# Column sums of squares in a hybrid encoder: fp32 products against split float32r ones

## The chip, the cores and the metric

The kernel runs on one core of a Trainium2 chip, all in float32 or float32r (fp32 data that TensorE multiplies in one pass, with fewer bits of mantissa). The metric is the time of one execution on the device in microseconds (us); for the kernel before it is the median of three runs, for the profiles a single execution.

## What is computed

An encoder trunk of two layers over 512 tokens of 1024 features. Cut to what matters:

```python
def rmsnorm(x, w):
    y = x * lax.rsqrt(jnp.mean(x * x, axis=-1, keepdims=True) + 1e-6)
    return y * w

for i in range(2):
    h = rmsnorm(x, norm_mix[i])
    x = x + (gla_mixer(h) if i == 0 else attn_mixer(h))
    x = x + conv_ffn(rmsnorm(x, norm_ffn[i]))

# inside attn_mixer: 8 query heads and 2 key heads of 128 features
q = apply_rope(rmsnorm(q, q_norm)); k = apply_rope(rmsnorm(k, k_norm))
```

So there are four norms over the 1024 features of a token (GLA's, the first feed-forward's, the attention's, the second feed-forward's), and norms over the 128 features of each query and key head. Each needs the sum of squares over features for every token. The output is x after both layers.

## The kernel before, in words

Activations lie with features on the 128 partitions and the 512 tokens along the free dimension: x is eight tiles of 128x512. Every weight product is made from a high and a low part: a value a is copied into float32r (hi, on ACT), the rest a - hi is written as float32r (lo, on DVE), and three one-pass products, hi by hi, hi by lo and lo by hi, take the place of an fp32 one (mm3, L555 to 559, and the loops at L610, L667, L735, L1155). The loops run over chunks of 128 input features (k or KC), output tiles, and, in most of the feed-forward, over the seven products of a Strassen scheme (L1155).

Four stages follow one another: gla, ffn(0), attention, ffn(1). What TensorE, ACT, DVE and GpSimd (POOL) do, and in which order, is written as one Python program; the framework underneath puts every instruction into its engine's queue when the kernel is built. It goes by the place in the program (earlier is more urgent) and by its own estimates of durations: an instruction is placed when its inputs are ready by the estimate and its engine is free, and another that is ready can be placed ahead of one that isn't. On the chip each queue then runs in the order so fixed. The kernel pushes the order where it matters with a table of actions by step (PLAN, tick), issue_after and high_priority. Tiles of one tag share a few buffers; the tag sq has three of 128x512, and a new tile waits until a buffer is free.

A norm (class Norm, L501 to 553) works in pieces. square (L529 to 536) squares a chunk of x on ACT (L531) and adds it on DVE (L535) into the tile ss, an sq buffer. tokens (L538 to 547) sums ss over the partitions: four blocks of 128 tokens are the stationary operand, one after the other, and a column of 1/1024 (ones, L476) is the moving one, so that 128 tokens' means come out as one column of PSUM (tile ms, L543). Then EPS is added on DVE (L487), the power -1/2 is taken on POOL (L491), and DVE copies it (rtok, L547). rows (L549 to 553) turns it into a tile R with one value for each token along the free dimension by four transposes (L498). In GLA tokens is the action T at step f3 and rows the action R at f6, while products for the first q and k tiles run.

In the attention (from L1441) the heads of q and k are made in pairs by roped (L1464 on): 8 + 8 steps of products into two PSUM tiles A and B, squares of both on ACT (L1470, L1471, tiles qa and qb in sq buffers), their sum on DVE (L1472), the rotation on DVE and POOL (L1480, L1499, L1500), and scale_tok (L1453 to 1462), which sums these squares (of both halves of a head's features) over the 64 partitions of each of the two heads: four blocks are stationary, and a two-column matrix bd with 1/128 in the upper half of one column and in the lower half of the other moves (tile hs, L1457). EPS is added on DVE (L1459) and POOL takes the root (L1461). The k pair runs first, then the norm's tokens, then the first q pair; the other three q pairs are spread over the steps of the attention's main loop, among scores (tile s), transposes of the probabilities (tile pt, L1623), products with v (po) and the output projection (op, L610). av (L584) are v's own products.

So the sums over partitions are made in 4 norms x 4 blocks and in 5 head pairs x 4 blocks, all with fp32 operands.

Of the kernel before, what the change touches and what calls it, by code (L numbers as in the profile page):

```python
# [8 lines left out]
F32 = mybir.dt.float32  # L9
F32R = mybir.dt.float32r  # L10
U8 = mybir.dt.uint8
AF = mybir.ActivationFunctionType
ALU = mybir.AluOpType

P = 128
S = 512
D = 1024
KC = D // P
NT = S // P
# [3 lines left out]
QH, HD = 8, 128  # L23
# [95 lines left out]
def hybrid_encoder_kernel(  # L119
# [23 lines left out]
    pe, act, dve, pool, sync = nc.tensor, nc.scalar, nc.vector, nc.gpsimd, nc.sync  # L143
    mm = pe.matmul

    cp = ctx.enter_context(tc.tile_pool(name="cp", bufs=1))
    sp = ctx.enter_context(tc.tile_pool(name="sp", bufs=1))
# [5 lines left out]
    def nm(s):  # L153
        uid[0] += 1
        return f"{s}{uid[0]}"
# [3 lines left out]
    def bank(tag, n):  # L159
        return pp.tile([P, S], F32, tag=tag, bufs=PS[tag], name=nm(n))  # L160
# [10 lines left out]
    def tiny(w, n, tag="tiny"):  # L171
        return sp.tile([P, 8], F32, tag=tag, bufs={"tiny": 36, "tiny2": 4}[tag], name=nm(n))[:, :w]
# [300 lines left out]
        mm(warm[:, :P], two[:, :P], two[:, P : 2 * P], start=i in (0, WARM - 8), stop=i in (WARM - 9, WARM - 1))  # L473
    halfneg = cp.tile([P, 8], F32, name="halfneg")
    dve.tensor_copy(halfneg, warm[:, :8])
    ones = cp.tile([P, 1], F32, name="ones")  # L476
    dve.memset(ones, 1.0 / D)
    bd = cp.tile([P, 2], F32, name="bd")
    dve.memset(bd, 0.0)
    dve.memset(bd[0:64, 0:1], 1.0 / HD)  # L480
    dve.memset(bd[64:128, 1:2], 1.0 / HD)

    def rsqrt_eps(src, w, n, scale=None, tag="tiny"):

        t = tiny(w, n, tag)
        if scale is None:
            dve.tensor_scalar(t, src, EPS, None, ALU.add)  # L487
        else:
            dve.tensor_scalar(t, src, scale, EPS, ALU.mult, ALU.add)
        r = tiny(w, n, tag)  # L490
        pool.tensor_tensor(r, t, halfneg[:, :w], ALU.pow)  # L491
        return r

    def bcast_rows(cols):

        ps = bank("po", "bc")
        for j in range(NT):
            pe.transpose(ps[:, j * P : (j + 1) * P], cols[j], ident)  # L498
        return ps

    class Norm:  # L501
# [36 lines left out]
        def tokens(self):  # L538

            assert self.done == KC  # L540
            ps = bank("po", "ms")
            for j in range(NT):
                mm(ps[:, j : j + 1], self.ss[:, j * P : (j + 1) * P], ones, start=True, stop=True)  # L543
            self.ms = ps[:, :NT]
            r = rsqrt_eps(self.ms, NT, "rtok")
            self.rtok = cp.tile([P, NT], F32, name=nm("rtok"))
            dve.tensor_copy(self.rtok, r)  # L547
# [92 lines left out]
    def gla(norm, nxt):  # L640
# [349 lines left out]
        def roots(h):  # L990

            oss = tiny(4, "oss")
            for s in range(NT):
                junk = tmp("sq", "junk", DV)
                act.activation(junk, O[h][:, s * DV : (s + 1) * DV], AF.Square, accum_out=oss[:, s : s + 1])
            ORS[h] = rsqrt_eps(oss, NT, "ors", 1.0 / DV)
# [444 lines left out]
    def attention(norm, nxt):  # L1441
# [11 lines left out]
        def scale_tok(sq, by, keep):  # L1453

            ps = bank("acc", "hs")
            for j in range(NT):
                mm(ps[:, 2 * j : 2 * j + 2], sq[:, j * P : (j + 1) * P], bd, start=True, stop=True)  # L1457
            t = tiny(8, "hs", "tiny2")
            dve.scalar_tensor_tensor(by_two(t), by_two(ps[:, :8]), by, by_block(eps[by]), ALU.mult, ALU.add)  # L1459
            o = cp.tile([P, 8], F32, name=nm(keep))  # L1460
            pool.tensor_tensor(o, t, halfneg, ALU.pow)  # L1461
            return o

        def roped(i, wcol, by, keep, tag="acc"):  # L1464
# [17 lines left out]
            turned(0)  # L1482
            yield
            sc = scale_tok(qa, by, keep)
            yield
            turned(1)
# [72 lines left out]
        ps = [bank("acc" if j < 2 else "pt", "av") for j in range(NT)]  # L1559
# [8 lines left out]
        for j in range(NT):  # L1568
            sl = slice(j * 256, (j + 1) * 256)
# [83 lines left out]
        for t in range(len(blocks) + LAG2):  # L1653
# [10 lines left out]
            if t >= LAG + 1 and (t - LAG) % 2 == 1 and t < len(blocks) + LAG:  # L1664
                h, j = blocks[t - LAG]
# [110 lines left out]
```

## Time and profile before

| what | value |
|---|---|
| median of 3 runs | 1073.53 us (1072.96 to 1073.98) |
| the profiled execution, its own time | 1074.18 us |
| its span, first to last instruction | 1072.5 us |
| granted TensorE clock | 1.00 |

The span lacks about 1.7 us of start and end that the time has. In the profile, PE is TensorE's matmuls, PEld its weight loads, DVE VectorE, ACT ScalarE, POOL GpSimd, SP the queue of SyncE; L543 is line 543 of the kernel. A row of the timeline has start and length in us, the engine, the line, the operation, output and inputs, shapes, and in brackets the idle time ahead of it and what ended that. A row with x8 stands for eight instructions in a run, from the first one's start to the last one's end. Ends of matmuls are modelled, and matmuls overlap: of two in a row, the distance of their starts is what counts. A row of waits has the total in us, how often, and the longest. Rows by tile have the shortest, the median and the longest duration in ns and the first and the last start in us.

### The profile page before, as it was taken

The numbers are of one execution on the slowest core, as the hardware profiler recorded it, in microseconds if no ns is written. First come the engines' busy times: TensorE is split into PE (matmuls) and PEld (weight loads), VectorE is DVE, ScalarE is ACT, GpSimd is POOL, SyncE is SP. The second block draws the span as 40 slices with busy tenths as digits, with TensorE's granted clock in tenths as the row PEclk, the third lists the DMA queues.
The fourth block names the chain that finished last, engine by engine and source line by source line (L and its number), as shares of the span: only waits on it lengthen the run. The fifth ranks groups of instructions, "written<-read, shape, count | busy, mean of one in ns | idle before, by whom it ended". The sixth has DMA issues, their size and how long they took to land.

```text
span 1072.5 us, 18688 instructions
## 1 busy us (share of the span) xinstructions
PE 1064.6 (99%) x7176; PEld 981.3 (91%) x7176; DVE 941.0 (88%) x1423; ACT 784.0 (73%) x1252; POOL 157.0 (15%) x169
## 2 busy tenths in 40 slices
PE   9999999999999999999999999999999999999998
PEld 8888988888999999999988888788899999999997
DVE  7998968878999999999985578787899999999996
ACT  8679665767886778776893677675888777876783
POOL 0212112021100110010015243001201021001000
PEclk9999999999999999999999999999999999999999
DMA  8744447666564874474768565486756487456562
GB/s 304 179 127 103 117 146 255 225 137 130 144 151 121 207 184 127 121 176 123 233 171 204 122 202 167 149 263 143 145 128 159 117 195 198 128 129 156 149 194 83
DMA packets 75323, 174.57 MB, mean 163 GB/s; under 512 B 6881, under 2 KB 7393, under 8 KB 75233
## 3 DMA queue, kind: packets, MB, share of 16 engines
q1 hardware_dynamic: 50624, 114.23, 31.8%
q0 software_dynamic: 19712, 50.60, 27.1%
q10 hardware_dynamic: 4896, 8.55, 2.2%
q8 instruction: 56, 0.92, 0.4%
q14 instruction: 35, 0.28, 0.1%
HBM read 124.85 MB, written 14.68 MB: 130 GB/s over the span
## 4 chain that ended last, share of the span: by engine, by line
PE 98%; ACT 1%; DVE 1%; DMA 0%; issue 0%; DVEq 0%; ACTq 0%
PE r L1155 53%; PE op L610 8%; PE vg L735 7%; PE up L558 3%; PE up L557 3%; PE up L559 3%; PE kq L667 2%; PE A L557 1%; PE A L559 1%; PE A L558 1%; PE B L557 1%; PE B L558 1%; PE B L559 1%; PE av L584 1%; PE pt L1623 1%; PE o L981 1%
## 5 line engine op out<-in xcount | busy, mean ns | idle before, releaser
L1155 PE MATMUL r<-xt,wh 128*128 128x256 f32 x1152 | 208.0, 282 | 0.0
L1155 PE MATMUL r<-gu,wh 128*128 128x256 f32 x1120 | 202.0, 283 | 0.0
L377 DVE TENSOR_TENSOR wl<-raw,wh 128x1024 fp32r<-128x1024 f32 x146 | 176.4, 1219 | 19.3 <-ACT wh L376 18.8
L1155 PEld LDWEIGHTS r<-xt,wh 128*128 128x128 f32 x1152 | 178.9, 190 | 0.2
L376 ACT ACTIVATE wh<-raw 128x1024 fp32r<-128x1024 f32 x146 | 151.1, 1051 | 33.6 <-PE vg L735 6.9
L1155 PEld LDWEIGHTS r<-gu,wh 128*128 128x128 f32 x1120 | 173.7, 191 | 1.1 <-ACT r L1224 0.3
L1155 PE MATMUL r<-xt,wl 128*128 128x256 f32 x576 | 162.8, 283 | 0.0
L1155 PE MATMUL r<-gu,wl 128*128 128x256 f32 x560 | 156.7, 283 | 0.0
L1155 PE MATMUL r<-nh,wh 128*128 128x256 f32 x432 | 122.5, 284 | 0.0
L1155 PE MATMUL r<-nh,wl 128*128 128x256 f32 x432 | 122.0, 283 | 0.0
L1155 PE MATMUL r<-nl,wh 128*128 128x256 f32 x432 | 121.7, 282 | 0.0
L1155 PEld LDWEIGHTS r<-xt,wl 128*128 128x128 f32 x576 | 109.7, 191 | 0.0
L1155 PEld LDWEIGHTS r<-gu,wl 128*128 128x128 f32 x560 | 106.3, 191 | 0.0
L1155 PEld LDWEIGHTS r<-nh,wh 128*128 128x128 f32 x432 | 82.1, 190 | 0.6
L1155 PEld LDWEIGHTS r<-nl,wh 128*128 128x128 f32 x432 | 82.1, 190 | 0.1
L1155 PEld LDWEIGHTS r<-nh,wl 128*128 128x128 f32 x432 | 82.1, 190 | 0.0
L376 ACT ACTIVATE wh<-sum 128x1024 fp32r<-128x1024 f32 x56 | 59.2, 1057 | 24.0 <-DVE sum L346 17.6
L610 PE MATMUL op<-oT,wh 128*128 128x512 f32 x256 | 72.6, 393 | 0.0
L377 DVE TENSOR_TENSOR wl<-sum,wh 128x1024 fp32r<-128x1024 f32 x56 | 68.3, 1219 | 3.8 <-ACT wh L376 3.8
L326 ACT ACTIVATE wh<-raw 128x1024 fp32r<-128x1024 f32 x46 | 48.3, 1051 | 18.0 <-PE A L558 6.7
L346 DVE TENSOR_TENSOR sum<-raw,raw 128x1024 f32<-128x1024 f32 x50 | 60.9, 1218 | 0.0
L610 PEld LDWEIGHTS op<-oT,wh 128*128 128x128 f32 x256 | 47.4, 188 | 9.7 <-ACT oT L1020 0.3
(304 smaller groups left out, 2579.3 us busy)
## 6 DMA issues: line engine op xcount, KB each, us to landing
raw<-in_w_up_dram SPq DMA_DIRECT2D x78, 512.0 KB, 5.2
raw<-in_w_down_dram SPq DMA_DIRECT2D x44, 512.0 KB, 4.1
wl<-raw POOLq DMA_DIRECT2D x20, 512.0 KB, 5.4
wl<-in_w_up_dram POOLq DMA_DIRECT2D x20, 512.0 KB, 6.6
ring<-p ACTq DMA_DIRECT2D x32, 256.0 KB, 2.4
xw<-in_xw_dram SPq DMA_DIRECT2D x8, 512.0 KB, 6.8
raw<-in_w_v_dram SPq DMA_DIRECT2D x8, 512.0 KB, 4.8
raw<-in_w_g_dram SPq DMA_DIRECT2D x8, 512.0 KB, 4.0
```

Of the source, the lines that this page charges most:

```text
L326: act.activation(hi, r, AF.Copy)
L346: dve.tensor_tensor(fold(e), t3[:, :S].rearrange("p (o n) -> p o n", o=1).to_broadcast([P, 2, S]), fold(tiles[0]), ALU.add)
L376: act.activation(hi[:, sl], a, AF.Copy)
L377: dve.tensor_tensor(lo[:, sl], a, hi[:, sl].bitcast(F32), ALU.subtract)
L557: mm(ps, wh, mh, start=start, stop=False, **kw)
L558: mm(ps, wh, ml, start=False, stop=False, **kw)
L559: return mm(ps, wl, mh, start=False, stop=stop, **kw)
L584: mm(ps[j][:, :width], hl[k][i == 2][:, j * P : (j + 1) * P], (wl if i == 1 else wh)[:, sl], start=k == 0 and i == 0, stop=k == KC - 1 and ...
L610: W.op = mm(pss[ng][n], wt[:, sl], mv, start=k == late[0][0] and i == 0, stop=k == late[-1][-1] and i == 2)
L667: mm(ps[t], (wl if i == 1 else wh)[:, kk * S + t * P : kk * S + (t + 1) * P], norm.hl[k][i == 2], start=k == 0 and i == 0, stop=k == KC - ...
L735: last = mm(ps[j], m[:, js], w[:, sl], start=i in (1, 7, 2) and p == 0 and a == 0, stop=i in (4, 2, 3) and p == 3 and a == 2, skip_group_c ...
L1155: mm(dst, w[:, sl], m, start=start and j == 0 and a == 0, stop=j == len(pairs) - 1 and a == 2, skip_group_check=True)
```

## The change

The columns ones and bd become parts of one float32r tile (a row of fp32 constants, bd0, is copied into it by one more operation on DVE; ones has two equal columns now). A new function column_sums splits a tile of sums of squares into high and low parts, in two sq buffers, and sums the two parts by two float32r products into the same two columns of PSUM, instead of one fp32 product. scale_tok uses it for all five head pairs; Norm.tokens uses it for the norms of even index, which are GLA's (0) and the attention's (2). The feed-forward norms (1 and 3) keep fp32 products. The means of a norm now lie in every second column of ms.

```diff
-    ones = cp.tile([P, 1], F32, name="ones")
-    dve.memset(ones, 1.0 / D)
-    bd = cp.tile([P, 2], F32, name="bd")
-    dve.memset(bd, 0.0)
-    dve.memset(bd[0:64, 0:1], 1.0 / HD)
-    dve.memset(bd[64:128, 1:2], 1.0 / HD)
+    bd0 = cp.tile([P, 4], F32, name="bd0")
+    dve.memset(bd0[:, 0:2], 1.0 / D)
+    dve.memset(bd0[:, 2:4], 0.0)
+    dve.memset(bd0[0:64, 2:3], 1.0 / HD)
+    dve.memset(bd0[64:128, 3:4], 1.0 / HD)
+    bd = cp.tile([P, 4], F32R, name="bd")
+    dve.tensor_copy(bd, bd0)
+    ones, bd = bd[:, 0:2], bd[:, 2:4]
...
+    def column_sums(ps, a, by):
+
+        hi, lo = (sp.tile([P, S], F32R, tag="sq", bufs=3, name=nm(n)) for n in ("sh", "sl"))
+        act.activation(hi, a, AF.Copy)
+        dve.tensor_tensor(lo, a, hi.bitcast(F32), ALU.subtract)
+        for j in range(NT):
+            for t in (hi, lo):
+                mm(ps[:, 2 * j : 2 * j + 2], t[:, j * P : (j + 1) * P], by, start=t is hi, stop=t is lo)
...
             ps = bank("po", "ms")
-            for j in range(NT):
-                mm(ps[:, j : j + 1], self.ss[:, j * P : (j + 1) * P], ones, start=True, stop=True)
-            self.ms = ps[:, :NT]
+            if self.idx % 2:
+                for j in range(NT):
+                    mm(ps[:, 2 * j : 2 * j + 1], self.ss[:, j * P : (j + 1) * P], bd0[:, 0:1], start=True, stop=True)
+            else:
+                column_sums(ps, self.ss, ones)
+            self.ms = ps[:, : 2 * NT : 2]
...
             ps = bank("acc", "hs")
-            for j in range(NT):
-                mm(ps[:, 2 * j : 2 * j + 2], sq[:, j * P : (j + 1) * P], bd, start=True, stop=True)
+            column_sums(ps, sq, bd)
```

## The prediction

> **What bounds the kernel now.** I read the page's busy times first, then its chain of waits, then the waits of TensorE, and then the stretches around the seven places that the change touches.
>
> ```profile
> PE 1064.6 (99%) x7176; PEld 981.3 (91%) x7176; DVE 941.0 (88%) x1423; ACT 784.0 (73%) x1252; POOL 157.0 (15%) x169
> PE 98%; ACT 1%; DVE 1%; DMA 0%; issue 0%; DVEq 0%; ACTq 0%
> ```
> ```profile
> PE warm L473 <- DVE bd L479: 1.3, 1, 1.3
> ```
>
> TensorE is busy for 1064.6 us, 99% of the span, the chain that ended last is TensorE's own work for 98%, and the longest wait of its matmuls is the 1.3 us before its very first one. So a microsecond of TensorE work that goes is very nearly a microsecond off the time, a microsecond in which TensorE waits is one on it, and work on VectorE (DVE) or ScalarE (ACT) counts only where TensorE has to wait for it.
>
> **TensorE: what goes and what comes.** The sums by fp32 products appear in the trace under the tiles ms and hs:
>
> ```profile
> L543 PEld LDWEIGHTS ms<-ones,sq x32: 186/192/192, 25.9 to 736.7; 128*128 128x128 f32 x32
> ```
> ```profile
> L1457 PEld LDWEIGHTS hs<-bd,qa x40: 186/192/192, 572.2 to 655.3; 128*128 128x128 f32 x40
> ```
>
> The program writes 4 products for each of four norms and 4 for each of five heads' sums; the trace has 32 and 40 weight loads, so one fp32 product is two loads with two matmuls. Two of the four norms and all five heads' sums are changed: 16 + 40 = 56 load-and-matmul pairs go. In their place come 7 x 4 blocks x 2 halves = 56 one-pass products. If each of these is one pair, the number of loads is what it was, and only the price of one can differ. That price shows around the k heads' sum:
>
> ```profile
> 572.24 1.08 PEld L1457 LDWEIGHTS hs<-bd,qa 128*128 128x128 f32 x8
> 573.25 0.19 PEld L557 LDWEIGHTS A<-xhl,wh 128*128 128x128 f32 x1
> 573.36 0.19 PEld L558 LDWEIGHTS A<-xhl,wh 128*128 128x128 f32 x1
> 573.60 0.19 PEld L559 LDWEIGHTS A<-xhl,wl 128*128 128x128 f32 x1
> ```
> ```profile
> 572.47 0.95 PE L1457 MATMUL hs<-bd,qa 128*128 128x2 f32 x8
> 573.28 0.49 PE L557 MATMUL A<-xhl,wh 128*128 128x512 f32 x1
> 573.60 0.40 PE L558 MATMUL A<-xhl,wh 128*128 128x512 f32 x1
> 573.84 0.40 PE L559 MATMUL A<-xhl,wl 128*128 128x512 f32 x1
> ```
>
> Two columns are no work: eight matmuls of two columns take 0.81 us from the first start (572.47) to the next product's (573.28), 0.10 each, and the loads' own starts, 572.24 to 573.25, with the first of them made ahead beside a 512-column product, give (573.25 - 572.47) / 7 = 0.11. So these sums are paid by their weight loads. The next two loads, at 573.25 and 573.36, are of float32r weights (the page prints them as f32; the code makes wh in float32r), and behind idle columns they too stand 0.11 apart; the matmul at 573.28 holds TensorE for 0.32 instead of the 0.24 of its successor (573.60 to 573.84) because its weights come that late. Their recorded length, 0.19, is that of the fp32 loads above. A float32r load thus costs what an fp32 load costs, 0.11 us, and 56 x 0.11 = 6.2 us go and 6.2 us come: zero.
>
> Nearest row that speaks for less:
>
> ```profile
> L1623 PEld LDWEIGHTS pt<-ident,ring x128: 137/139/147, 608.8 to 699.4; 128*128 128x128 f32 x128
> L1623 PE MATMUL pt<-ident,ring x128: 222/246/282, 609.0 to 699.5; 128*128 128x128 f32 x128
> ```
> ```profile
> 608.99 0.79 PE L1623 MATMUL pt<-ident,ring 128*128 128x128 f32 x8
> ```
>
> Float32r transposes load in 0.139 and pass at (0.79 - 0.25) / 7 = 0.08 us (0.25 is the recorded length of the last). At that price 56 x 0.03 = 1.7 us would be saved. The bounds of this term are therefore -1.7 and 0, and I take 0, since the new products are plain ones, like L557's, and not transposes. (Nothing shows a plain float32r product narrower than 256 columns; what it would be if the narrow one weren't one pass is a rival below.)
>
> The Trainium skill, page "TensorE: Matmul & The Clock Gate", section "LDWEIGHTS (loading the stationary operand)", puts a load at its columns divided by 1.2, which for 128 is about 107 ns whatever the type. The 0.11 us of both kinds here agrees. Its section "Weight-path perf modes" says that the fast weight load is on for 128 weights of any type but fp32; by that, the float32r loads here ought to be the quicker ones, and the rows at 573.25 and 573.36 don't bear it out.
>
> **ACT and DVE: two operations more at each place.** Each of the seven sums gets a copy on ACT into float32r and a subtraction on DVE, both of 128x512 from SBUF. The same two operations are made for each half of k:
>
> ```profile
> 580.29 0.63 ACT L1506 ACTIVATE k<-ry 128x512 fp32r<-128x512 f32 x1 [3.07 <-DVE ry L1524]
> ```
> ```profile
> 581.67 0.69 DVE L1507 TENSOR_TENSOR k<-ry,k 128x512 fp32r<-128x512 f32 x1
> ```
>
> 7 x 0.63 = 4.4 us on ACT and 7 x 0.69 = 4.8 us on DVE, on engines that TensorE hardly waits for: by themselves, nothing. What counts is that they stand in line: the products of a sum can begin 0.63 + 0.69 = 1.3 us later than now, or more if the copy queues behind other ACT work. Engines work through their queues in a fixed order, so a product that isn't ready holds up all of TensorE's products behind it. Place by place, DVE's last sum and TensorE's start:
>
> ```profile
> 22.85 0.69 DVE L535 TENSOR_TENSOR sq<-sq,sq 128x512 f32<-128x512 f32 x1
> ...
> 27.14 0.16 DVE L487 TENSOR_SCALAR rtok<-ms 128x4 f32<-128x4 f32 x1 [3.27 <-PE ms L543]
> ```
> ```profile
> 26.16 0.95 PE L543 MATMUL ms<-ones,sq 128*128 128x1 f32 x8
> ```
> ```profile
> 561.00 0.68 DVE L535 TENSOR_TENSOR sq<-sq,sq 128x512 f32<-128x512 f32 x1
> ```
> ```profile
> 567.43 0.95 PE L543 MATMUL ms<-ones,sq 128*128 128x1 f32 x8
> ```
>
> GLA's norm is ready at 23.5 and used at 26.2, and DVE sits idle for 3.27 us in between; the attention's is ready at 561.7 and used at 567.4. Slack 2.6 and 5.7 us against 1.3: nothing. If that cover were gone, each would cost up to 1.3.
>
> ```profile
> 569.82 0.69 DVE L1472 TENSOR_TENSOR qa<-qa,qb 128x512 f32<-128x512 f32 x1
> ...
> 583.50 0.68 DVE L1472 TENSOR_TENSOR qa<-qa,qb 128x512 f32<-128x512 f32 x1
> ```
> ```profile
> 584.24 1.05 PE L1457 MATMUL hs<-bd,qa 128*128 128x2 f32 x8
> 585.16 0.49 PE L584 MATMUL av<-wh,xhl 128*128 128x256 f32 x2
> ```
> ```profile
> 609.11 0.68 DVE L1472 TENSOR_TENSOR qa<-qa,qb 128x512 f32<-128x512 f32 x1
> ```
> ```profile
> 609.85 1.05 PE L1457 MATMUL hs<-bd,qa 128*128 128x2 f32 x8
> ```
> ```profile
> 609.52 1.04 ACT L326 ACTIVATE wh<-raw 128x1024 fp32r<-128x1024 f32 x1
> ```
> ```profile
> 627.73 0.69 DVE L1472 TENSOR_TENSOR qa<-qa,qb 128x512 f32<-128x512 f32 x1 [0.73 <-ACT qb L1471]
> ```
> ```profile
> 628.98 0.95 PE L1457 MATMUL hs<-bd,qa 128*128 128x2 f32 x8
> ```
> ```profile
> 653.38 0.69 DVE L1472 TENSOR_TENSOR qa<-qa,qb 128x512 f32<-128x512 f32 x1 [0.49 <-ACT qb L1471]
> ```
> ```profile
> 654.63 0.95 PE L1457 MATMUL hs<-bd,qa 128*128 128x2 f32 x8
> ```
> ```profile
> PEld hs L1457 <- DVE qa L1472: 0.5, 2, 0.3
> ```
>
> Here it is tight. The k heads' sum is ready at 570.5 and used at 572.5, 2.0 us later; the first and second q pairs' are used the moment they are ready (584.2 and 609.8), and TensorE waited 0.5 us in these two together; the third and the last have 0.6 us each. Were the products left where they are in TensorE's order, the waits would be 0, 1.3, 1.3 (2.0 if the copy first sits out the ACT work at 609.52 to 610.5), and 0.7 twice. But the order is laid out again when the kernel is built, by estimated times, and behind each of these places stand products that need nothing of it (av at 585, A at 573). So the sums will move back in the order by the estimated delay, and what is left is the error of the estimate. Now there is one hand-over, DVE to TensorE, and the error cost 0.5 us over the five; with three hand-overs (DVE, ACT, DVE, TensorE) I take three times that, 1.5: **+1.0 us**. Bounds: 0 and the 1.3 + 2.0 + 0.7 + 0.7 = 4.7 of the order kept.
>
> What is late behind a later sum: the root on POOL and the scales. For k this is covered:
>
> ```profile
> 571.99 3.26 POOL L1500 TENSOR_TENSOR ry<-rt,rt 64x512 f32<-64x512 f32 x2 [0.87 <-DVE rt L1480]
> 575.33 1.67 POOL L1461 TENSOR_TENSOR ksc<-hs,halfneg 128x8 f32<-128x8 f32 x1
> ```
>
> POOL is busy with the rotation until 575.3 anyway, so k's root wouldn't start sooner. Halves are kept in the three sq buffers: at the attention's norm they fill all three, and the squares of k wait for one; the norm's sum is freed as soon as its low half is made, so I cost that at zero (if it isn't freed in time, k's squares wait for the products at 567.43 and k's sum comes later by about their length, 1 us, inside the 2.0 at hand). The start, with the constants made in float32r, has a copy more on DVE:
>
> ```profile
> 4.79 0.43 DVE L374 CAST wh<-xw 128x512 fp32r<-128x512 f32 x1 [3.31 <-DMA xw<-in_xw_dram]
> ```
>
> DVE is idle for 3.31 us there until the first input lands: zero. The feed-forward norms keep their fp32 products; a stride of two in four columns of PSUM is nothing.
>
> **Sum.** 0 (loads) + 0 (norms) + 1.0 (heads) = +1.0 us. The profiled execution took 1074.18 us, 0.65 above the median of 1073.53; 1074.18 + 1.0 = 1075.2 for such an execution, 1074.5 for the median. A difference under 0.2% (2.1 us) is about what a measurement of this kernel can't tell from none, so the forecast is "no change".
>
> **Rivals.** *Narrow float32r loads are quick.* If a load that nothing wide follows cost half of an fp32 one, as one pass against two might suggest, 56 x 0.055 = 3.1 us would go with TensorE's count the same: with waits of 0 to 1.0, 1070.4 to 1071.4, faster. (It is what the skill's fast weight load would look like here.) For it: float32r transposes do load quicker (0.139 against 0.19). Against it: the two plain float32r loads 0.11 apart. Chance 0.16.
>
> *The order is kept and TensorE waits at the heads.* The copy and the subtraction sit behind softmax work on ACT and DVE, the products are not moved far enough, and TensorE stands still with all its work behind them: +2.2 to +4.7, so 1075.7 to 1078.2, slower. It decides from 0.45 us of wait in each of the five places. For it: two of five waited already, with less in the way. Against: the placement is made anew and there is other work. Chance 0.25.
>
> *The products aren't one pass.* If a two-column float32r product were still two pairs, 56 pairs more would come, +6.2 and the waits: 1080. Against: every float32r product in the trace is one pair (128 transposes, 128 loads). Chance 0.03.
>
> **Numbers.** The forecast has 0.56: 1073.5 to 1075.6, the waits between 0 and their threshold. Faster by over 0.2%: the first rival and a small share for a luckier order, 0.18. Slower: second and third, 0.28. Within: 0.54. The range goes from 1071.0, inside the first rival, to 1077.2, two thirds into the second.
>
> **What would show it.** Right: TensorE's count stays at 7176 loads; eight products of a sum still take 0.8 us; ACT gains 7 and DVE 7 operations and a few for the constants; waits of hs for its low half of some tenths. Wrong: eight products in 0.5 us or less (loads are quicker), 56 loads more (not one pass), or waits of hs over 2 us in all; a changed time with none of these would mean that the new order moved waits elsewhere.

## The result and the profile after

| kernel | median of its runs | its runs | profiled execution, span |
|---|---|---|---|
| before, beside it | 1073.76 us | 1072.96 to 1074.32, 6 runs | 1074.18, 1072.5 us |
| after | 1077.88 us | 1076.24 to 1079.39, 6 runs | 1079.39, 1077.7 us |

The ratio is 1.0037, with a 95% interval from 1.0027 to 1.0047: 4.1 us slower. The forecast was 1074.5 and its range ended at 1077.2. The profiled execution is the slowest of the six; of its 5.2 us over before's, some 1.5 are that one execution's own. One of the twelve executions of split_all_mended, further down, took 3696.37 us and is not in that run's ratio.

The page after, its busy times and the first line of its chain of waits:

```profile
PE 1065.6 (99%) x7176; PEld 981.0 (91%) x7176; DVE 951.3 (88%) x1431; ACT 787.6 (73%) x1259; POOL 157.3 (15%) x169
PE 91%; DMA 3%; ACT 2%; DVE 2%; issue 1%; SPq 0%; ACTq 0%; DVEq 0%; POOLq 0%
```

TensorE's loads are 7176 as before and its busy time grew by 1.0 us only. What changed is the chain: where 98% of it was TensorE's own work, 91% is now, and DMA, ACT and DVE have the rest. TensorE waits more; it doesn't work more. The waits of its matmuls, longest first (who waited, for whom, total, times, longest):

```profile
PE warm L473 <- DVE bd L478: 1.3, 1, 1.3
PE kq L573 <- DMA wl<-raw: 1.2, 1, 1.2
PE pt L1636 <- DMA ring<-p: 1.0, 1, 1.0
PE A L573 <- DMA wl<-raw: 1.0, 1, 1.0
PE hs L503 <- ACT sh L499: 0.7, 1, 0.7
...
PE pt L1636 <- DVE rc L1610: 0.5, 1, 0.5
PE hs L503 <- DVE sl L500: 0.5, 1, 0.5
PE z L828 <- DVE rst L804: 0.5, 1, 0.5
```

The first was there before; so was one of 0.9 for ring<-p. New are kq and z (GLA, at 40.6 and 44.3 us), A (560.0), two of hs (613 to 616) and pt for rc (673). Held against the same matmuls of the trace before, the starts fall behind by 1.9 us up to 46 us, by 1.2 at 560, by 1.4 at the second pair of query heads and by 0.7 at 673.

**GLA.** The sums themselves, on TensorE, and what made them late, on DVE:

```profile
28.44 0.17 PE L503 MATMUL ms<-bd,sh 128*128 128x2 f32 x1
...
29.71 0.17 PE L503 MATMUL ms<-bd,sl 128*128 128x2 f32 x1
```
```profile
26.60 0.69 DVE L500 TENSOR_TENSOR sl<-sq,sh 128x512 fp32r<-128x512 f32 x1
...
30.59 0.16 DVE L489 TENSOR_SCALAR rtok<-ms 128x4 f32<-128x4 f32 x1 [2.90 <-PE ms L503]
```

The low half is ready at 27.3, 3.7 us after the norm's sum (23.6) and not 1.3, since its two operations queued on ACT and DVE; TensorE takes it up 2.4 us later still; EPS is added at 30.59 where it was 27.14. TensorE waits for none of this. But POOL's queue, after and before:

```profile
27.21 0.87 POOL L365 DMA_DIRECT2D wl<-raw  x1 [5.36 <-ACT wl L325]
30.83 1.21 POOL L493 TENSOR_TENSOR rtok<-rtok,halfneg 128x4 f32<-128x4 f32 x1 [2.76 <-DVE rtok L489]
32.02 0.91 POOL L365 DMA_DIRECT2D wl<-raw  x1
```
```profile
27.39 1.42 POOL L491 TENSOR_TENSOR rtok<-rtok,halfneg 128x4 f32<-128x4 f32 x1 [5.64 <-DVE rtok L487]
28.78 1.82 POOL L365 DMA_DIRECT2D wl<-raw  x2
```

Before, the root ran first and both DMAs that add up w_kq's low halves went out by 30.6. After, one goes ahead of the root and the other stands behind it until 32.02. On it hang a product (kq) and, through the raw buffer that it frees, w_v's third load on SP, which went out in one row with the first two in the kernel before (after, then before):

```profile
32.33 0.81 SPq L217 DMA_DIRECT2D raw<-in_w_v_dram  x2
...
40.63 0.80 SPq L217 DMA_DIRECT2D raw<-in_w_v_dram  x2
```
```profile
33.50 3.60 SPq L217 DMA_DIRECT2D raw<-in_w_v_dram  x3
```

The rank rows (rf, copied into rst) come late as well. DVE makes them at 38.83 where it was 32.76, behind work that stood after them, and ACT's queue changed its order too. Before, the copy rst ran well ahead of the copy of a w_v load; now it stands behind such a copy, and that one waits for its load (before, then after):

```profile
35.23 0.61 ACT L789 ACTIVATE rst<-rf 128x512 fp32r<-128x512 f32 x1
...
41.99 1.06 ACT L376 ACTIVATE wh<-raw 128x1024 fp32r<-128x1024 f32 x1 [3.97 <-DMA raw<-in_w_v_dram]
```

```profile
41.15 1.06 ACT L376 ACTIVATE wh<-raw 128x1024 fp32r<-128x1024 f32 x1 [4.84 <-DMA raw<-in_w_v_dram]
42.11 0.62 ACT L803 ACTIVATE rst<-rf 128x512 fp32r<-128x512 f32 x1
```
```profile
40.62 0.50 PE L573 MATMUL kq<-xhl,wl 128*128 128x512 f32 x1 [1.17 <-DMA wl<-raw]
...
44.33 0.47 PE L828 MATMUL z<-rst,gst 128*128 128x512 f32 x1 [0.46 <-DVE rst L804]
```

The last two rows are TensorE's: a wait for the low half itself, and one for the rank rows before the first product of the gates (z). The copy at 41.15 can't wait for the third load, which SP had sent only half a microsecond before (these loads take 5.2 us to land, the median of seven). So in this trace the rows are late by their place in the queues, and the low half costs through kq alone.

**The second query pair.** TensorE, DVE and POOL:

```profile
613.48 0.27 PE L503 MATMUL hs<-bd,sh 128*128 128x2 f32 x1 [0.73 <-ACT sh L499]
...
615.49 0.27 PE L503 MATMUL hs<-bd,sl 128*128 128x2 f32 x1 [0.48 <-DVE sl L500]
615.62 0.25 PE L503 MATMUL hs<-bd,sh 128*128 128x2 f32 x1
615.73 0.25 PE L503 MATMUL hs<-bd,sl 128*128 128x2 f32 x1
```
```profile
614.07 1.36 DVE L500 TENSOR_TENSOR sl<-qa,sh 128x512 fp32r<-128x512 f32 x1
615.36 1.49 DVE L1611 TENSOR_SCALAR p<-p,rc 128x512 f32<-128x512 f32 x1
```
```profile
613.51 1.36 POOL L1512 TENSOR_TENSOR ry<-rt,rt 64x512 f32<-64x512 f32 x1
614.95 1.61 POOL L1513 TENSOR_TENSOR ry<-rt,rt 64x512 f32<-64x512 f32 x1
```

The first product waits for the high part, the second for the low part: the build had not moved them far enough. The subtraction takes 1.36 us where 0.68 is usual (0.69 in GLA's, above), while POOL rotates; that rotation stood behind the root before and now runs ahead of it.

### The profile page after: what moved, and what is told of

It reads as the page before. It is cut to its first block, busy times and chain, and to the rows that moved or that the text cites. A ratio compares the mean times of both kernels' runs of the same rounds, so it can differ in the third digit from the quotient of the medians.

```text
span 1077.7 us, 18705 instructions
## 1 busy us (share of the span) xinstructions
PE 1065.6 (99%) x7176; PEld 981.0 (91%) x7176; DVE 951.3 (88%) x1431; ACT 787.6 (73%) x1259; POOL 157.3 (15%) x169
## 4 chain that ended last, share of the span: by engine, by line
PE 91%; DMA 3%; ACT 2%; DVE 2%; issue 1%; SPq 0%; ACTq 0%; DVEq 0%; POOLq 0%
PE r L1169 51%; PE op L624 8%; PE vg L749 7%; PE up L572 3%; PE up L571 3%; PE up L573 3%; DMA wl<-raw 1%; PE av L598 1%; PE A L573 1%; PE B L571 1%; PE B L573 1%; PE B L572 1%; PE A L571 1%; PE A L572 1%; DMA raw<-in_w_v_dram 1%
```

## The experiments

The theory after the result: TensorE's own work is unchanged, and the time went into waits that the longer way to the root makes, in GLA behind the root on POOL, at the heads at the products themselves. The rivals: a cost of the parts' added work wherever they stand; the rank rows in GLA; the hand-over through ACT, or POOL's rotation, at the heads. Each run stands beside runs of the kernel before on the same chip; "alone" means that the other sums are fp32 products as before.

| run | median, us | before, us | ratio, 95% interval |
|---|---|---|---|
| gla_norm_only | 1075.64 | 1074.10 | 1.0013, 1.0004 to 1.0022 |
| attn_norm_only | 1074.08 | 1074.10 | 0.9999, 0.9990 to 1.0008 |
| heads_only | 1076.55 | 1074.10 | 1.0028, 1.0019 to 1.0037 |
| constants_only | 1073.97 | 1074.10 | 0.9999, 0.9991 to 1.0008 |
| gla_rank_rows_urgent | 1076.87 | 1073.89 | 1.0029, 1.0018 to 1.0040 |
| heads_high_on_dve | 1076.75 | 1073.89 | 1.0025, 1.0016 to 1.0034 |
| heads_rounded | 1071.44 | 1073.89 | 0.9977, 0.9968 to 0.9986 |
| norms_rounded | 1073.07 | 1073.89 | 0.9994, 0.9985 to 1.0003 |
| gla_norm_lows_first | 1077.65 | 1074.45 | 1.0030, 1.0018 to 1.0041 |
| heads_root_ahead | 1078.00 | 1074.45 | 1.0030, 1.0018 to 1.0043 |
| heads_sums_late | 1075.59 | 1074.45 | 1.0011, 1.0002 to 1.0019 |
| all_rounded | 1070.90 | 1074.45 | 0.9965, 0.9952 to 0.9977 |
| gla_lows_and_scan | 1074.19 | 1073.99 | 1.0004, 0.9995 to 1.0013 |
| gla_lows_scan_rows | 1073.65 | 1073.99 | 0.9995, 0.9987 to 1.0004 |
| split_all_mended | 1075.95 | 1073.99 | 1.0018, 1.0009 to 1.0026 |

**The change in four parts.** Which of the places loses?

```diff
-            if self.idx % 2:
+            if self.idx not in (0,):      # gla_norm_only; (2,): attn_norm_only; (): the other two
...
-            column_sums(ps, sq, bd)       # as it is in heads_only
+            for j in range(NT):
+                mm(ps[:, 2 * j : 2 * j + 2], sq[:, j * P : (j + 1) * P], bd0[:, 2:4], start=True, stop=True)
```

> Split products in GLA's norm alone; the attention's norm and the five head sums keep fp32 products. Theory A (each place costs by its own waits): the profile of the changed kernel loses 1.9 us by 46 us, 1.3 of it where a k product waits for a low half that POOL's queue issues behind the norm's root, and 0.6 where the first gate waits for rst. So +1.9 us against before, with those two waits in the trace, and nothing after. Theory B (the loss comes from the order as a whole being laid out anew, wherever a part of the change is made): waits appear in the attention too, or the GLA ones vanish; the sum is not 1.9.

> Split products in the attention's norm alone. Theory A: 0.0 us, since its sum is ready some 5 us before TensorE uses it; the wait of 1.1 us for a low half's transfer at the attention's first products is a late landing of that one profiled execution. Theory C (that wait belongs to the change): +1.1 us and the same wait in this trace.

> Split products for the five head sums alone; all four norms keep fp32 products. Theory A: +1.4 us where the second head pair's halves are late (0.9 for the high half, 0.6 for the low one), and up to 0.8 where the probabilities' transposes are late near the end of the attention: +1.4 to +2.2 us. Theory B: not within that.

> All sums in fp32 products, but the constants in one tile with the copy into float32r, and the means of a norm in every second column. Theory A: 0.0 us. Theory B: some of the 4 us are here already, by a new order.

By the ratios, GLA's norm loses 1.4 us and the heads 3.0; the attention's norm and the constants lose nothing that can be measured. The sum, 4.4, is the whole change's 4.1 within its interval. The heads' 3.0 is more than the 1.4 to 2.2 expected; in the trace of heads_only the starts fall behind by 1.4 us at the second pair and 0.7 at 670, and the rest is not in that execution. The wait for A at 560 us is not in the run of the attention's norm, but waits of 0.2 to 1.2 us stand at the same place in five later traces, one of them with GLA's norm alone split; what sets it isn't shown. In GLA's alone, the wait for the rank rows shows, longer than in the whole change:

```profile
42.84 0.47 PE L828 MATMUL z<-rst,gst 128*128 128x512 f32 x1 [1.11 <-DVE rst L804]
```

The other wait expected there, of kq for the low half, is not in this trace. The DMA went out at 31.35, behind the root too, and the load that waits for its buffer at 38.15, 6.8 us later; in the trace after it was 8.6 (32.02 to 40.63). This execution (1073.96) is the fastest of eleven that reach up to 1077.16, so one trace doesn't show all of the median's loss.

**GLA: is it the rank rows?** The rank rows were moved ahead in the build's order of urgency.

```diff
+        def rows_first(_):
+            with tc.high_priority(100):
+                rank_rows(0)
...
-"r": rank_rows
+"r": rows_first
```

> As the run with GLA's norm alone split, but the action that makes rst out of the ranks (rank_rows) is given a higher priority when the order is laid out, which puts its DVE product ahead of seven other DVE operations again. Theory A1 (GLA's loss is rst: a norm that is 1.3 us later made the order push rst behind other DVE work and behind an ACT copy that waits for a weight's transfer, and the first gate waits for rst): the wait before the first gate is gone and the time is that of before, 0 to +0.4 us. Theory A2 (the loss is the low half queued behind the root on POOL): +1.4 us as with the norm alone.

It didn't get better: the loss by the ratio is 3.1 us, against 1.4 with GLA's norm as it is. The rows are in time now, ACT copies them at 35.10, and TensorE waits at the second gate product instead, for ACT's work on the first gate, which is queued behind the copy of a w_v load:

```profile
42.56 1.06 ACT L376 ACTIVATE wh<-raw 128x1024 fp32r<-128x1024 f32 x1 [4.65 <-DMA raw<-in_w_v_dram]
...
44.09 0.68 ACT L841 ACTIVATE gm<-z,gconst 128x512 f32<-128x512 f32 x1
```
```profile
44.82 0.50 PE L828 MATMUL z<-rst,gst 128*128 128x512 f32 x1 [1.20 <-ACT gm L841]
```

So the rank rows alone aren't the cause. Here the load is late: SP sent the second and third at 37.03, when the low half had landed, where it was 36.30 before, and the copy starts at 42.56, where it was 41.99. That is about half of the 1.2.

**GLA: is it the low half behind the root?** Both accumulating DMAs go ahead of the root on POOL.

```diff
+                self.flushed = getattr(self, "flushed", 0) + 1
+                with tc.high_priority(1000) if self.flushed <= 3 else ExitStack():
                     pool.dma_start(lo.bitcast(F32) if same else lo, r, accum_op=ALU.add)
```

> GLA's norm alone is split (heads and the other norms stay fp32 products), and both accumulating DMAs that make w_kq's low halves are put ahead of the root on POOL's queue; in the run with the norm alone the second stood behind the root and was issued at 31.35 us (29.7 in the kernel before). Theory A2 (the late root holds back the second low half, that holds its raw buffer, that holds w_v's third load, and ACT's copies stand behind the copy of that load): the third load goes out at 36 to 37 us and not at 38 to 40, and the time falls from +1.4 us to between 0 and +0.5 (1073.9 to 1074.5). Theory A3 (the norm's own chain, its root and rank rows, is what comes too late): still +1.0 to +1.6, with a wait of over 1 us before the first gate product.

The waits of kq and z are gone, and the kernel still loses 3.2 us. One wait has taken their place (a row of the waits, and DVE's queue):

```profile
PE vg L751 <- DVE wl L379: 2.1, 1, 2.1
```
```profile
55.81 1.22 DVE L858 TENSOR_TENSOR_SCAN ga<-gconst,gm 128x512 f32<-128x512 f32 x1 [3.47 <-issue]
56.95 1.20 DVE L379 TENSOR_TENSOR wl<-raw,wh 128x1024 fp32r<-128x1024 f32 x1
```

DVE stands still for 3.47 us in front of the scan of the gates and makes w_v's low half only then, though its high half was copied on ACT from 51.77 to 52.8. The build had put the scan ahead of it; in the kernel before, it comes behind. What the wait cost beyond its own length stands in the last section.

So this order was put right as well (with the fourth sum of w_v's parts on DVE more urgent, the build lays the scan behind that low half again), without and with the rank rows of rows_first:

```diff
+                self.adds = getattr(self, "adds", 0) + 1
+                with tc.high_priority(1000) if self.adds in (4,) else ExitStack():
                     dve.tensor_tensor(r, r, plus, ALU.add)
```

> GLA's norm alone split; both low halves of w_kq ahead of the root on POOL, and on VectorE the low half of w_v ahead of the scan's wait, as in the kernel before. Theory A2 (low half behind the late root holds the raw buffer and w_v's third load): neither the 1.3 us wait before the first gate product nor the 2.1 us wait for w_v's low half is there, and the time is 0 to +0.5 us from before. Theory A3 (the norm's chain to the rank rows is what is late): still +1.0 or more, with a wait for the rank rows before the first gate product.

> As gla_lows_and_scan, with the rank rows ahead on VectorE too. Theory A2: no different from gla_lows_and_scan by more than 0.4 us. Theory A3: this one comes back to 0 to +0.5 where the other keeps +1.0 or more.

> The kernel of gla_lows_scan_rows once more, as a second profile of it: the same waits where they are the order's, others where they are the landing of a DMA.

With the two orders the loss is 0.4 us with an interval from -0.5 to 1.4; with all three it is -0.5 (-1.4 to 0.4). With these orders GLA's split costs nothing that can be measured. The same orders were not put into the kernel before; should they gain something there, the split costs as much. The two medians differ by 0.54, more than the 0.4 allowed for the low half as the only cause, but their intervals overlap. In the profiled execution without the rank rows, whose time of 1075.74 is among the longest of its runs, their old wait is back, though SP sends the third load early there (three in one row from 32.73 to 35.61),

```profile
PE z L832 <- DVE rst L808: 1.6, 1, 1.6
```

and both profiled executions of the kernel with them (1072.99 and 1074.02 us) have no wait of a matmul between 20 and 70 us. In the first of them SP issues w_v's third load in one row with the first two again:

```profile
33.14 2.81 SPq L217 DMA_DIRECT2D raw<-in_w_v_dram  x3
```

So the rank rows' wait does not need the late load, and the low half and the rows are two causes. Whether the rows still have a share in the median once the low half is ahead, these runs can't tell.

**The heads: which hand-over?** High part on DVE instead of ACT, in heads_only.

```diff
-        act.activation(hi, a, AF.Copy)
+        dve.tensor_copy(hi, a)
```

> As the run with the heads alone split, but the high half is copied on DVE and not on ACT. Theory H1 (the second head pair's products wait because the copy queues on ACT behind other copies, and each hand-over from engine to engine adds): the 0.9 us wait for the high half goes and the low half comes sooner; +1.0 to +2.0 us instead of +3.0. Theory H2 (the loss is DVE's own extra work in the attention): no better than +3.0 us.

No change (2.7 us by the ratio): TensorE now waits 1.1 us for the high part from DVE where it waited 0.7 for ACT's.

**The heads: rotation ahead of the root, or the wait at the products?** (H1 is from here on TensorE's wait at the products, whichever engine it waits for.) Two edits of heads_only: the rotation laid behind the root again, and the products, EPS and the root two yields later in the program, with the parts' two operations written right behind the sum of the squares. (In the traces of the second pair these two come when they came: 609.71 and 610.98 us, in heads_only 609.68 and 610.95.)

```diff
+            roped.root = pool.tensor_tensor(o, t, halfneg, ALU.pow).ins
...
+                with tc.issue_after(roped.root):
                     sub.tensor_tensor(res[e][0:64, :], t[0][r, :], t[1][r, :], ALU.subtract)
```
```diff
             dve.tensor_tensor(qa, qa, qb, ALU.add)
+            parts = high_low(qa)          # the copy and the subtraction of column_sums
...
-            sc = scale_tok(qa, by, keep)
             yield
             turned(1)
             yield
+            sc = scale_tok(qa, by, keep, parts)      # only the products, EPS and the root
             turned(2)
```

> Heads alone split; POOL's rotation is laid behind the root of its heads, as in the kernel before, and not in front of it. Theory H2 (POOL's rotation, now ahead of the root, runs beside the low part's subtraction and makes it 1.36 us long instead of 0.68, and delays the root): the subtractions are 0.7 us, and +3.0 us falls to between +0.5 and +1.5. Theory H1 (TensorE waits for the parts at the products whatever POOL does): still +2.5 to +3.5.

> Heads alone split; the products that sum the parts stand one step later in TensorE's order for the last three pairs of q (3 to 18 products later), so that they cannot wait for the parts; the parts are made where they were. Theory H1 (the direct wait at the products is the loss): no wait of an hs product over 0.2 us, and +3.0 us falls to between 0 and +1.0. Theory H3 (the loss comes through what the late root holds up on POOL, the low halves of the query weights and the rotation): still +2.5 or more, since the root comes later still.

With the rotation behind the root the subtractions are short again (five of 0.67 to 0.68 us), the 0.5 of wait for the low part is gone, and the kernel still loses 3.2 us: what was won there is lost at other places of the softmax (waits of heads_root_ahead from 540 us on),

```profile
PE po L571 <- ACT pth L1640: 1.1, 1, 1.1
PE pt L1637 <- DVE rc L1611: 0.8, 1, 0.8
```

so the slow subtraction is seen, but it isn't the loss. (POOL's rotation now runs beside other work of DVE: a scaling of p at 614.85 takes 1.32 us where 0.48 is usual. What such meetings cost in all was not taken apart.) With the sums later, the loss falls from 3.0 to 1.2 us, and no product of hs waits any more:

```profile
PE pt L1642 <- DMA ring<-p: 1.9, 1, 1.9
...
PE pt L1642 <- DVE ptl L1646: 1.1, 1, 1.1
PE A L578 <- DMA wl<-raw: 0.9, 1, 0.9
```

That is 0.2 over the 1.0 that the theory of the wait at the products allowed, and far from the 2.5 of the other. What is left is in the transposes of the probabilities (1.9 for ring where it was 0.9, 1.1 for ptl where there was none). One thing wasn't taken apart: in this order a low half of the query weights also comes ahead of the third pair's root on POOL (632.95 against 635.02 us; in heads_only it went out at 638.68, behind the root), so that a part of the 1.8 may be due to that.

**The whole change with all these orders.** The diffs of gla_lows_scan_rows and heads_sums_late together, on the kernel after.

> The whole change (GLA's norm, the attention's norm, all heads split), with the orders of gla_lows_scan_rows and the heads' sums one step later in TensorE's order. Theory: the split costs TensorE nothing, and its loss is in the orders alone: +0.5 to +1.5 us (0 to 0.5 from GLA, 1.1 from the heads as measured with later sums). If the parts themselves cost (ScalarE's and VectorE's added work): +3 or more.

It loses 1.9 us, 1.0 to 2.8: about half of the change's loss is gone. That is 0.4 more than the theory of the orders allowed and 1.1 less than the rival asked for; what is left shows, as in heads_sums_late, in the transposes (waits of 1.9 for ring and 1.1 for ptl) and at A (1.2). Whether these are orders too, or a cost of the parts in the attention's full ACT and DVE, stays open.

**Only the high part.** The sum of squares is rounded: DVE's last addition writes float32r, and four one-pass products follow. The low part is left out of the computation, and with it the copy and the subtraction.

```diff
-            dve.tensor_tensor(qa, qa, qb, ALU.add)
+            qr = sp.tile([P, S], F32R, tag="sq", bufs=3, name=nm("qr"))
+            dve.tensor_tensor(qr, qa, qb, ALU.add)
...
+                to = sp.tile([P, S], F32R, tag="sq", bufs=3, name=nm("sr")) if self.done == KC - 1 else self.ss
-                dve.tensor_tensor(self.ss, self.ss, q, ALU.add)
+                dve.tensor_tensor(to, self.ss, q, ALU.add)
```

> The head sums leave out the low part: DVE's last addition writes the squares' sum in float32r, and four one-pass products a sum follow; the norms keep fp32 products. No operation is added to the chain, and 20 load-and-matmul pairs of 0.11 us fewer are issued. If loads are what these sums cost and waits are what the split cost: -2.2 us against before, with 7156 matmuls. If the one-pass products themselves were slow or the float32r addition: 0 or above.

> All four norms leave out the low part: the last addition of squares is written in float32r and four one-pass products a norm follow; the heads keep fp32 products. 16 pairs of 0.11 us fewer: -1.8 us against before if nothing in the chain changes. If any new order about GLA's norm brings the waits of the split version: 0 or above.

> All four norms and all heads sum one rounded square by one-pass products: the last addition writes float32r into a buffer of its own, and the low part is left out, so each sum has 4 load and product pairs where the fp32 product has 8. 36 pairs fewer by 0.11 us: 4.0 us if all of it lies on TensorE's path, 3.2 by the sum of the two halves as measured (2.4 and 0.8): 1069.9 to 1070.8.

The heads give 2.5 us, the norms 0.6 (a change between -1.6 and 0.3) where 1.8 were expected, and all of it 3.8 (2.5 to 5.2). The norms' trace has two waits that before's has not, of 0.5 and 0.4. The page of all_rounded:

```profile
PE 1060.6 (99%) x7140; PEld 977.1 (91%) x7140; DVE 941.6 (88%) x1424; ACT 784.0 (73%) x1252; POOL 157.3 (15%) x169
```

It has 36 loads fewer, PE 4.0 us less, and DVE and ACT are where they were before. This version beats both kernels, at the price of sums of squares rounded once to float32r's mantissa.

## Why the prediction was wrong

- **Loads, zero: right.** 7176 in both kernels; in the row of hs products above they follow one another at 0.11 us, high and low parts alike. So neither the first rival (quick loads) nor the third (not one pass) came about, and the 36 pairs of all_rounded gave 3.8 us where 36 x 0.11 = 4.0.
- **Added work on ACT and DVE by itself, nothing: borne out for the norms, open for the heads.** With the orders mended GLA's split is at 0.9995, and the attention's norm is at 0.9999; at the heads part of the loss has no cause yet. The sizes: ACT grew by 3.6 us, where 4.4 were forecast, and DVE by 10.3, where 4.8 were. The seven subtractions are 5.5 of that; DVE's four rotations now all run beside POOL's (1.6 to 1.8 us each, where the median was 0.68) and some scalings of p take up to 1.5.
- **The attention's norm, nothing; the start, k's root and the sq buffers, nothing: right**, by attn_norm_only and constants_only, and by the waits, none of which names k's sum.
- **GLA's norm, "Slack 2.6 ... against 1.3: nothing": this step failed.** It measured 1.4 us. The slack was taken up to TensorE's start and against the bare lengths of the two operations. In the trace the low half came 3.7 us after the sum, since both stood in queues, the products 2.4 after that, and TensorE indeed didn't wait for them. What was late stood behind the root: a low half of w_kq on POOL, for which kq waited 1.2 us, and the rank rows, which the build now put behind a copy on ACT, for which z waited 0.5. (Where the rows were put ahead, the load of w_v that waits for the low half's buffer was late instead.) The prediction asked "what is late behind a later sum" for k's heads only and never went through POOL's queue in GLA.
- **The heads, +1.0: mis-sized.** Measured 3.0. That the sums would move back and leave the error of the estimate was right in kind: two waits of hs, 0.7 and 0.5, are 1.2. The rest isn't at these products: with the parts late and the order laid out anew, pt waits for rc, and the rotation changes places with the root. With the sums later the loss is 1.2; what that rest is made of stays open. The bounds given, 0 to 4.7, held it.
- **The rivals.** The time, 1077.88, lies in the range of the second, and by its place (the heads) it is the nearest; but the order was not kept, and a third of the loss is GLA's, which no case had.
- **"Waits of hs over 2 us" as the sign of failure** didn't come; the sentence behind it did, that a changed time without it "would mean that the new order moved waits elsewhere".

## What to carry to other kernels

When an operation gets a longer chain in front of it, its slack is not that to its own start: list what stands behind it in every queue that its result passes (here POOL's root, then a DMA, a product that needs it, a buffer and a load) and take the smallest. Where a build lays out queues by estimates, a longer chain changes orders that have nothing to do with it, and one order mended by hand can move another (gla_norm_lows_first lost 3.2 us that way), so look at the same place of all queues before and after, and mend them together. Splitting one fp32 product into two one-pass products has the same number of loads, so it can't gain where narrow products are paid by their loads; leaving a pass out can.

## What the runs showed of the hardware that was not expected

**A wait of 2 us can cost nearly as much again.** TensorE around its wait in gla_norm_lows_first, in stretches (from and to, length, busy time and count of PE, PEld, DVE, ACT and POOL, then the granted clock, the DMA share and GB/s):

```profile
56.00:58.20 2.20, 0.15 (x1) 0.00 (x0) 2.20 (x4) 0.00 (x0) 0.00 (x0) 1.00 0.00 0
58.20:60.00 1.80, 1.80 (x5) 1.42 (x6) 1.80 (x5) 0.61 (x1) 0.00 (x0) 0.58 0.00 0
60.00:62.00 2.00, 2.00 (x7) 1.55 (x6) 1.93 (x4) 2.00 (x4) 0.00 (x0) 0.53 0.00 0
62.00:64.00 2.00, 2.00 (x10) 1.62 (x9) 2.00 (x4) 2.00 (x3) 0.00 (x0) 1.00 0.00 0
```

After the wait the granted clock was 0.58 and 0.53 for 3.8 us, which costs 1.8 x 0.42 + 2.0 x 0.47 = 1.7 us on top of the wait. In heads_sums_late the wait of 1.9 us, at 686 to 688, left the clock as it was:

```profile
686.00:688.00 2.00, 0.14 (x2) 0.07 (x1) 1.85 (x5) 0.59 (x2) 0.00 (x0) 1.00 1.00 316
688.00:690.00 2.00, 2.00 (x13) 1.73 (x14) 0.83 (x2) 1.58 (x4) 0.00 (x0) 1.00 0.03 11
```

The Trainium skill, page "TensorE: Matmul & The Clock Gate", part 1 ("The HAM clock gate"), has the array fall to half its clock after an idle window of about 3.4 us, a window that runs freely. The half clock agrees, and the 3.8 us are near that window; here a wait of 2.1 us was enough, in one trace, and one of 1.9 was not, in two (the other is that of split_all_mended).

**VectorE beside POOL.** The subtraction that began at 614.07 took 1.36 us: POOL's operation of 613.51 ended at 614.87, and 0.56 of the row is left after that. The next one on VectorE, from 615.36, took 1.49 instead of 0.48 and ended at 616.85, just behind POOL's at 616.56. The Trainium skill, page "SBUF — State Buffer", section "SBUF: two separate sides", says that a GpSimd operation and some of VectorE's (such as those with two inputs in SBUF) take a shared pair of ports for a whole instruction, and the other waits; these ends agree with it.
